# Second product of a feed-forward layer: from the planner's order to an order written out by hand, on VectorE, ScalarE and the load queue

## The chip, the cores and the metric

One NeuronCore of one Trainium2 chip runs the whole program. The metric is the device time of one execution in microseconds (us); of several executions the median is given. Engines are named as in the profile: PE (TensorE, matrix multiplications), PEld (its weight loads), DVE (VectorE), ACT (ScalarE), POOL (GpSimd) and SP (SyncE, which here only issues DMAs).

## The reference

The program is one layer of a sequence model on 512 tokens of width 2048: a state-space branch and an attention branch, merged, and then a gated feed-forward. Only the feed-forward matters here:

```python
D_MODEL, SEQ, D_FF = 2048, 512, 5632          # float32 in and out
h = rms_norm(x, norm2_w[l], RMS_EPS)
x = x + (jax.nn.silu(h @ w_ffn_gate[l]) * (h @ w_ffn_up[l])) @ w_ffn_down[l]
```

The *first product* is `h @ w_ffn_gate` and `h @ w_ffn_up`; the *second product* is the multiplication by `w_ffn_down` (5632 x 2048).

## The kernel before, in words

**Arithmetic.** Each multiplication is done by seven smaller products of operands and weights (Strassen's scheme in Winograd's form), numbered 1 to 7. Each float32 value of operands and weights is split into a high part and a rest (`whi` on ACT by `activation(Copy)`, `wlo` on DVE by a subtraction), and high x high, high x rest, rest x high are added up in PSUM. The unit of work is a *chunk* (`chunk`, L1049): one 128x1024 piece of weight (512 KB), split by ACT and DVE, then 12 multiplications of 128x128 by 128x512 on PE (line L1055 in the profile). The split results rotate through three buffers each (`halves`).

Products 1, 2 and 3 read weight blocks as they are loaded, 7, 5, 6 and 4 sums of blocks. A place A of the weights runs through these forms: block (1,1) for product 1; plus (1,2), in place, for 5; plus (2,2) for 6; plus (2,1) for 4. The other blocks are called R (2,1), r (1,2) and Q (2,2); product 7 takes r + Q, made in place of r. A += r, r += Q, A += Q are additions on DVE over 128x1024 elements. A += R is an addition of two loaded pieces or a second load of (2,1) by POOL that adds to what lies in SBUF (`pool.dma_start(..., accum_op=ALU.add)`, called the *adding load* below).

**First product.** D_FF is cut into 11 units of 512 columns, u = 0 to 10. Unit 0 runs in `seven` (L1058). Units 1 to 10 run in `units` (L1232), whose order on PE, DVE and ACT is written out step by step (`tc.manual_schedule` for these three engines): in step s PE does chunk s, ACT and DVE split the weight of step s+2, and DVE makes the sums for step s+4. What a unit leaves behind is done in `post`, a table from step to calls. The load queue (SP) is not in that order: a planner that estimates times places its loads. The results of unit u are turned by four transposes on PE (`flip_act`), split and stored in DRAM (`make`, tensor `opd`, seven operands of 512 KB for each unit) as operands of the second product.

**Second product.** It runs in six blocks of `blocks`: unit 0 alone (n = 2), then the pairs (1,2) ... (9,10) (n = 4). Each block is run for two halves v of the output rows, so there are 12 passes: 2 of 7 chunks, 10 of 14 chunks, 154 chunks in all. A pass is one call of `seven`: for each product in the order 1, 2, 7, 5, 6, 3, 4 it calls `weights` (loads and sums), `split`, `chunk` and, at the product's last chunk, `done`, which adds the two PSUM banks of the product to sums in SBUF (`acc`; the keys 11, 57, x, 53, 74). Only PE is held in program order here (`manual_schedule(engines={PE})` from the caller); DVE, ACT and SP run in the order that the planner found. The slabs with the operands (`s7`: 1 and 7, `s3`: 2 and 5, `s4`: 6 and 3, `s2`: 4) are filled at the start of a block from `opd` by 7 loads for each unit (L1525). The places A, R, Q of a block are halves of two slabs (`self.E`, `self.A`) that change roles from block to block; r takes a buffer of the ring `raw` (three). For n = 4 A += R is an adding load, in both halves v.

**The end.** The last pass is accompanied by `final` (L1496): four transposes into a PSUM bank (`flips`, banks T and O in turn), an addition of the residual by DVE and the store of a tile of 256 KB. Half v = 0 has eight such tiles during the last pass, their residual loaded by an ACT-issued DMA; of v = 1 four stand around the last two chunks and four after them. In the last block the sum x is subtracted or added in `done` directly after product 6.

Line L1350 is the helper `load` (SP), L1334 the helper `add` (DVE), L499/L500, L530/L531 and L1301/L1306 the two halves of a split, L1369 the store to `opd`, L1280 and L1556 the adding loads of the first and second product, L1229 the transposes.

Of the kernel before, what the change touches and what calls it, by code (L numbers as in the profile page):

```python
# [41 lines left out]
class Block:  # L42
    def __init__(self, ctx, tc, a):
# [12 lines left out]
        self.fp = None  # L56
        self.hook = None
# [1166 lines left out]
    def flips(self, parts):  # L1224

        self.nf += 1
        tp = self.bank("TO"[self.nf % 2])
        for h, z in enumerate(parts):
            self.nc.tensor.transpose(tp[:, h * P:(h + 1) * P], z, self.ident)  # L1229
        return tp  # L1230

    def units(self, ops, block, load, stage, stages, flip_act, make):  # L1232

        nc = self.nc
        dve, add = nc.vector, lambda o, x, y: nc.vector.tensor_tensor(o, x, y, op=ALU.add)
        NU, A, E = DFF // T, self.A, self.E
        order = ((1, 2), (7, 5, 3, 6), (4,))
        S = [(u, i, c) for u in range(1, NU) for g in order for c in range(0, 8, 2) for i in g]  # L1240
        own = {1: ("lin", "lin"), 7: ("lin", "lin"), 2: ("S", "S"), 5: ("S", "S"), 3: ("T", "O")}
        st = [{} for _ in range(NU)]

        queue = [(u, k, m, c) for u in range(1, NU) for k, m, c in
                 [(2, 1, c) for c in range(0, 8, 2)] + [(k, 2, c) for c in range(0, 8, 2) for k in (1, 2)]]
        held, w, n = [None] * 5, {}, 0

        def loads():
            nonlocal n
            while queue and held[n % 5] is None:  # L1250
                key = queue.pop(0)
                p = n % 5
                t = E[:, 2 * p - 6:2 * p - 4] if p > 2 else self.wp.tile([P, 2, T], F32, tag="raw", bufs=3, name=self.uid("raw"))
                held[p] = key
                w[key] = load(t, block(*key))
                n += 1

        def give(*key):
            held[held.index(key)] = None

        base = lambda u, c: load(A[:, c:c + 2], block(u, 1, 1, c))
        src = lambda u, i, c: A[:, c:c + 2] if i in (1, 5, 6, 4) else w[(u, *{2: (2, 1), 7: (1, 2), 3: (2, 2)}[i], c)]

        def sums(u, i, c):
            a = A[:, c:c + 2]
            if i == 7:
                add(a, a, w[u, 1, 2, c])
                add(w[u, 1, 2, c], w[u, 1, 2, c], w[u, 2, 2, c])
            elif i == 6:
                add(a, a, w[u, 2, 2, c])  # L1270

        def taken(u, i, c):
            if i == 2:
                give(u, 2, 1, c)
            elif i == 7:
                give(u, 1, 2, c)
            elif i == 3:
                give(u, 2, 2, c)
            elif i == 6:
                nc.gpsimd.dma_start(A[:, c:c + 2], block(u, 2, 1, c).rearrange("(k p) c -> p k c", p=P), accum_op=ALU.add)  # L1280
            elif i == 4 and u + 1 < NU:
                base(u + 1, c)

        post, fill, hl = {}, {}, {}
        at = lambda s, f: post.setdefault(s, []).append(f)
        for u in range(1, NU):
            s0 = 28 * (u - 1)
            for j in range(4):
                fill[s0 + 4 + j] = lambda u=u, j=j, s=s0 + 5 + j: flip_act(u - 1, j, lambda f: at(s, f))

            for f, s in zip(make(u - 1, lambda f: at(self.slot + 1, f)), range(s0 + 9, s0 + 40, 3)):
                at(s, f)
        banks = {}
        for c in range(0, 8, 2):
            base(1, c)
        for s in range(-4, len(S) + 4):
            self.slot = s
            if 0 <= s + 2 < len(S):
                x = src(*S[s + 2])
                hl[s + 2] = self.halves()  # L1300
                nc.scalar.activation(hl[s + 2][0], x, AF.Copy)  # L1301
            for f in post.pop(s, ()):
                f()
            if 0 <= s + 2 < len(S):
                hi, lo = hl[s + 2]
                self.last = nc.vector.tensor_tensor(lo, x, hi.bitcast(F32), op=ALU.subtract)  # L1306
                taken(*S[s + 2])
            if s == -4:
                loads()
            if 0 <= s + 4 < len(S):  # L1310
                sums(*S[s + 4])
            loads()
            if 0 <= s < len(S):
                u, i, c = S[s]
                if c == 0:
                    banks[i] = [self.bank(t) for t in own[i]] if i in own else banks[{6: 1, 4: 7}[i]]
                self.chunk(banks[i], ops[i], *hl.pop(s), c, 8, i in own)
                if c == 6:
                    for tt in range(2):
                        st[u][f"p{i}", tt] = banks[i][tt]  # L1320
                    for d, name in stages[i]:
                        at(s + d, lambda u=u, name=name: stage(u, st[u], name))
                if s in fill:
                    fill[s]()
        assert not post and not queue

    def ffn(self, ops, steps, x2d, out):
# [158 lines left out]
        with tc.manual_schedule(engines={mybir.EngineType.PE, mybir.EngineType.DVE, mybir.EngineType.Activation}):  # L1486
            self.units(ops, block, load, stage, STAGES, flip_act, make)
        self.ring = 0
# [3 lines left out]
        big = [self.late.tile([P, 4, 2, T], F32, tag=t, name=self.uid(t)) for t in ("s6", "s9")]  # L1492
        more = self.late.tile([P, 2, 2, T], F32, tag="s8", name=self.uid("s8"))
        acc = [{**{q: big[v][:, q_i] for q_i, q in enumerate(("11", "57", "x", "53"))}, "74": more[:, v]}
               for v in range(2)]
        def final(v, m, j):  # L1496
            t = 8 * v + 4 * m + j
            js = slice(j * P, (j + 1) * P)
            parts = [acc[v][q][:, tt, js] for q in (("11", "74"), ("53", "57"))[m] for tt in range(2)]
            tp = self.flips(parts)  # L1500
            if v:
                o = st["x2"][:, t - 8]
            else:
                o = self.work()
                nc.scalar.dma_start(o, x2d[t])
            add(dve, o, o, tp)
            nc.sync.dma_start(out[t * P:(t + 1) * P, :], o)

        both = lambda f: [lambda: (f[0](), f[1]()), lambda: (f[2](), f[3]())]
        finals = lambda v, m: [lambda j=j: final(v, m, j) for j in range(4)]  # L1510


        A, R, Q, free = self.E[:, 0:4], self.A[:, 0:4], self.A[:, 4:8], self.E[:, 4:8]
        blocks = [[0]] + [[u, u + 1] for u in range(1, NU, 2)]
        for b, units in enumerate(blocks):
# [3 lines left out]
            for tag, two_ops in (("s7", (1, 7)), ("s3", (2, 5)), ("s4", (6, 3)), ("s2", (4,))):  # L1519
                t = self.slab(tag, (P, len(two_ops), 2, n, 256), F32R)  # L1520
                for h, i in enumerate(two_ops):
                    ops[i] = t[:, h]
# [71 lines left out]
        for f in finals(1, 0):  # L1594
            f()
# [38 lines left out]
```

## Time and profile before

| | us |
|---|---|
| median of 3 executions (lowest, highest) | 2568.91 (2568.69, 2571.08) |
| the profiled execution | 2570.0 |
| its span, first to last instruction | 2568.2 |

The mean granted TensorE clock of the profiled execution is 0.993. Read the profile with the stages in mind: the first product's hand-ordered part takes the stretch up to about 2115 us of the span, the second product what follows. A busy PE row means that a multiplication was in flight, and since they overlap (0.39 us each, one started every 0.23 us) short waits can be missing from it; the spacing of starts shows them.

### The profile page before, as it was taken

To read this page: it belongs to the slowest core of one execution; us is meant where nothing else is said; L and a number is where in the kernel's file an instruction comes from. 1 tells how busy PE (TensorE), PEld (TensorE's weight loads), DVE (VectorE), ACT (ScalarE), POOL (GpSimd) and SP (SyncE) were. 2 spreads that over 40 slices of the span, in tenths; PEclk is the share of its full clock that TensorE was granted. 3 is DMA by queue.
4 is the path that set the end of the run, shared out by engine and by line. 5 is a ranking of instruction groups with operands and counts; after the bars stand their busy time and mean duration, and the time that the engine had idled before them with its cause. 6 is when DMAs were issued, how large, how long until landed. Compare 5 with 4: busy or idle time off the path is not lost.

```text
span 2568.2 us, 32111 instructions
## 1 busy us (share of the span) xinstructions
PE 2513.2 (98%) x11655; PEld 2055.4 (80%) x11655; DVE 1927.1 (75%) x3046; ACT 1145.1 (45%) x1540; POOL 316.5 (12%) x491
## 2 busy tenths in 40 slices
PE   8999999999999999999999999999999999999999
PEld 6788887877787778888788888888888887788887
DVE  7888854476778775535678787888888888788788
ACT  4133443353555553323545555555455455333332
POOL 1022310000110110000001111111111111000000
PEclk9999999999999999999999999999999999999999
DMA  6545564666852434433666666666566687767774
GB/s 191 155 131 142 149 187 154 218 216 205 269 195 97 137 117 148 160 115 131 215 180 189 168 178 176 191 197 183 165 172 180 193 254 258 249 205 234 246 231 150
DMA packets 247567, 470.86 MB, mean 183 GB/s; under 512 B 42808, under 2 KB 47224, under 8 KB 247408
## 3 DMA queue, kind: packets, MB, share of 16 engines
q1 hardware_dynamic: 185328, 331.52, 39.9%
q0 software_dynamic: 49504, 133.04, 19.2%
q10 hardware_dynamic: 12576, 4.24, 0.8%
q8 instruction: 92, 1.51, 0.2%
q14 instruction: 67, 0.55, 0.1%
HBM read 399.38 MB, written 71.96 MB: 184 GB/s over the span
## 4 chain that ended last, share of the span: by engine, by line
PE 43%; issue 39%; POOL 6%; DVE 5%; DMA 5%; ACT 1%; POOLq 0%; ACTq 0%; SPq 0%; DVEq 0%
PE lin L522 30%; PE lin L1055 5%; POOL opd L1369 3%; DMA raw<-in_w_in_dram 3%; PE S L1055 2%; DVE wlo L531 2%; POOL s L1280 1%; POOL s L1556 1%; PE S L715 1%; ACT whi L530 1%; DVE raw L1088 1%; PE S L472 1%; PE O L745 1%; PE S L414 1%; PE S L476 0%
## 5 line engine op out<-in xcount | busy, mean ns | idle before, releaser
L1055 PE MATMUL lin<-whi,s 128*128 128x512 f32 x2400 | 770.1, 392 | 1.5 <-ACT whi L530 1.5
L522 PE MATMUL lin<-s,whi 128*128 128x512 f32 x2432 | 747.5, 397 | 17.3 <-ACT s L536 7.6
L522 PEld LDWEIGHTS lin<-s,whi 128*128 128x128 f32 x2432 | 455.3, 190 | 127.7 <-issue 14.8
L1055 PEld LDWEIGHTS lin<-whi,s 128*128 128x128 f32 x2400 | 452.3, 188 | 96.0 <-ACT whi L530 2.8
L1055 PE MATMUL lin<-wlo,s 128*128 128x512 f32 x1200 | 469.8, 392 | 7.1 <-DVE wlo L531 6.9
L522 PE MATMUL lin<-s,wlo 128*128 128x512 f32 x1216 | 456.0, 394 | 0.0
L1055 PE MATMUL S<-whi,s 128*128 128x512 f32 x1328 | 436.0, 393 | 0.2 <-ACT whi L530 0.2
L500 DVE TENSOR_TENSOR wlo<-raw,whi 128x1024 fp32r<-128x1024 f32 (+1 forms) x153 | 185.7, 1215 | 214.1 <-ACT whi L499 207.3
L1301 ACT ACTIVATE whi<-s 128x1024 fp32r<-128x1024 f32 x208 | 220.9, 1062 | 273.8 <-PE lin L1055 132.0
L1306 DVE TENSOR_TENSOR wlo<-s,whi 128x1024 fp32r<-128x1024 f32 x208 | 254.2, 1222 | 110.5 <-ACT whi L1301 109.6
L499 ACT ACTIVATE whi<-raw 128x1024 fp32r<-128x1024 f32 (+1 forms) x153 | 160.9, 1052 | 360.4 <-PE lin L522 323.5
L1055 PEld LDWEIGHTS S<-whi,s 128*128 128x128 f32 x1328 | 250.5, 189 | 52.3 <-ACT whi L530 0.6
L1055 PEld LDWEIGHTS lin<-wlo,s 128*128 128x128 f32 x1200 | 226.4, 189 | 58.2 <-DVE wlo L531 12.2
L522 PEld LDWEIGHTS lin<-s,wlo 128*128 128x128 f32 x1216 | 230.4, 190 | 48.4
L1055 PE MATMUL S<-wlo,s 128*128 128x512 f32 x664 | 260.5, 392 | 8.5 <-DVE wlo L531 8.5
L530 ACT ACTIVATE whi<-s 128x1024 fp32r<-128x1024 f32 x143 | 150.9, 1060 | 228.0 <-PE lin L1055 98.6
L531 DVE TENSOR_TENSOR wlo<-s,whi 128x1024 fp32r<-128x1024 f32 x143 | 174.2, 1221 | 64.3 <-ACT whi L530 63.9
L530 ACT ACTIVATE whi<-raw 128x1024 fp32r<-128x1024 f32 x118 | 124.0, 1058 | 161.3 <-DVE raw L1088 54.0
L1369 POOL DMA_DIRECT2D opd<-wk x154 | 95.2, 618 | 671.5 <-ACT wk L1379 509.8
L531 DVE TENSOR_TENSOR wlo<-raw,whi 128x1024 fp32r<-128x1024 f32 x118 | 142.1, 1220 | 32.6 <-ACT whi L530 32.1
L1055 PEld LDWEIGHTS S<-wlo,s 128*128 128x128 f32 x664 | 125.4, 189 | 37.0 <-DVE wlo L531 11.8
L1301 ACT ACTIVATE whi<-raw 128x1024 fp32r<-128x1024 f32 x72 | 76.5, 1062 | 98.5 <-PE lin L1055 54.2
(422 smaller groups left out, 2915.3 us busy)
## 6 DMA issues: line engine op xcount, KB each, us to landing
raw<-in_w_in_dram SPq DMA_DIRECT2D x175, 512.0 KB, 4.4
opd<-wk POOLq DMA_DIRECT2D x154, 256.0 KB, 4.2
s<-opd SPq DMA_DIRECT2D x77, 512.0 KB, 8.9
s<-in_w_ffn_down_dram SPq DMA_DIRECT2D x65, 512.0 KB, 6.4
s<-in_w_ffn_gate_dram SPq DMA_DIRECT2D x60, 512.0 KB, 4.8
raw<-in_w_ffn_up_dram SPq DMA_DIRECT2D x59, 512.0 KB, 3.8
s<-in_w_ffn_gate_dram POOLq DMA_DIRECT2D x44, 512.0 KB, 6.1
raw<-in_w_out_dram SPq DMA_DIRECT2D x32, 512.0 KB, 3.7
```

Of the source, the lines that this page charges most:

```text
L414: nc.tensor.matmul(mb[:, q * 32:(q + 1) * 32], w1[:, ri, q].rearrange("p k c -> p (k c)"), self.cd[:, ri, q].rearrange("p g c -> p (g c)") ...
L472: state = lambda ri, **kw: nc.tensor.matmul(y[:, q * P:(q + 1) * P], w2[:, ri, q].rearrange("p k c -> p (k c)"), sd[:, ri, q].rearrange("p ...
L499: nc.scalar.activation(hi[:, ks], raw[:, ks], AF.Copy)
L500: nc.vector.tensor_tensor(lo[:, ks], raw[:, ks], hi[:, ks].bitcast(F32), op=ALU.subtract)
L522: nc.tensor.matmul(acc[b], l, r, start=(k == 0 and i == 0), stop=(k == nk - 1 and i == 2))
L530: ins = self.nc.scalar.activation(hi, x, AF.Copy)
L531: self.nc.vector.tensor_tensor(lo, x, hi.bitcast(F32), op=ALU.subtract)
L715: nc.tensor.matmul(sp[m], qT[ms, h, i * P:(i + 1) * P], kT[ms, h, 0:W], start=True, stop=True)
L1055: self.nc.tensor.matmul(banks[tt], l, r[:, kk, :], skip_group_check=True, start=(own and k == 0 and q == 0), stop=(k == n - 1 and q == 2))
L1301: nc.scalar.activation(hl[s + 2][0], x, AF.Copy)
L1306: self.last = nc.vector.tensor_tensor(lo, x, hi.bitcast(F32), op=ALU.subtract)
L1369: pool.dma_start(opd[u, i - 1, :, h], hl[h].bitcast(F32))
```

## The change

`units` is removed. A new method `in_order` writes out the order of units 1 to 10 and of the whole second product as one list of steps, run by a new method `pipe`; SP joins PE, DVE and ACT under `manual_schedule`. Every place of the weights (A0 to A3, E0 to E3, r0 to r2) has a list of the loads that it will hold; `give` issues the next one where the place is free. The operands of a block are no longer brought together at its start, but slab by slab, one operand and then the other two steps later, as the products of the block before (its half v = 1) are done with the slab. In second-product blocks with n = 4, A += R is a DVE addition for v = 1 (except in the last block); it stays an adding load for v = 0 and in the last block. DVE's evacuation of a product stands one step after the product's end, before the split of that step; that of product 4 two steps after. The products 7 and 5 alternate by chunk, as 1 and 2 now do in the second product; 6, 3 and 4 come one by one. The transposes of the second product use the banks S, and the residual tiles for v = 0 are loaded by SP.

The diff, cut (`...` marks what is left out):

```diff
-        tp = self.bank("TO"[self.nf % 2])
+        tp = self.bank(self.flip_banks[self.nf % 2])
...
+    def pipe(self, steps, post):
+        nc, hl, ahead = self.nc, {}, {}
+        for s, t in enumerate(steps):
+            if t.get("sums"):
+                ahead.setdefault(s - t.get("lead", 4), []).append(t["sums"])
+        s = -4
+        while s < len(steps) or post:
+            self.slot = s
+            t = steps[s + 2] if 0 <= s + 2 < len(steps) else None
+            if t:
+                x = t["x"]()
+                hl[s + 2] = hi, lo = self.halves()
+                nc.scalar.activation(hi, x, AF.Copy)
+            for f in post.pop(s, ()):
+                f()
+            if t:
+                nc.vector.tensor_tensor(lo, x, hi.bitcast(F32), op=ALU.subtract)
+                t.get("taken", lambda: None)()
+            for f in ahead.pop(s, ()):
+                f()
+            if 0 <= s < len(steps):
+                t = steps[s]
+                self.chunk(t["banks"](), t["op"](), *hl.pop(s), t["c"], t["n"], t["own"])
+                t.get("after", lambda: None)()
+            s += 1
...
-        with tc.manual_schedule(engines={mybir.EngineType.PE, mybir.EngineType.DVE, mybir.EngineType.Activation}):
-            self.units(ops, block, load, stage, STAGES, flip_act, make)
+        with tc.manual_schedule(engines={mybir.EngineType.PE, mybir.EngineType.DVE, mybir.EngineType.Activation,
+                                        mybir.EngineType.SP}):
+            self.in_order(ops, block, stage, STAGES, flip_act, make, opd, x2d, out)
+    def in_order(self, ops, block, stage, stages, flip_act, make, opd, x2d, out):
...
+        def give(name):
+            if wait.get(name):
+                key, src = wait[name].pop(0)
+                tiles[key] = place(name)
+                nc.sync.dma_start(tiles[key], two(src))
...
+        def slabs(b, tag):
...
+            for h, i in enumerate(which):
+                ops2[b, i] = t[:, h]
+                def bring(h=h, i=i):
+                    for c, u in enumerate(blocks[b]):
+                        nc.sync.dma_start(t[:, h, :, 2 * c:2 * c + 2].bitcast(F32), opd[u, i - 1])
+                at(self.slot + 2, bring) if h else bring()
...
+        def final_at(s, v, m, j, d=3):
+            st = {}
+            at(s - d, lambda: st.update(f=final(v, m, j)))
+            at(s, lambda: st.update(f=st["f"]()))
+            at(s + 1, lambda: st["f"]())
...
+        e0, a0, a3, e2 = ("E0", "E1"), ("A0", "A2"), ("A3", "A1"), ("E2", "E3")
+        roles.append(dict(A=e0, R=a0, Q=a3))
+        role = [a0, a3, e0, e2]
+        for _ in range(3, 2 * len(blocks)):
+            roles.append(dict(zip("ARQ", role)))
+            role = [role[3], role[2], role[1], role[0]]
...
+                def sums2(b, v, i, c, n):
+                    x, r, q = (tiles[b, v, z, c] for z in "ArQ")
+                    if i == 7:
+                        add(x, x, r)
+                        add(r, r, q)
+                    elif i == 6:
+                        add(x, x, q)
+                    else:
+                        add(x, x, tiles[b, v, "R", c])
+                        give(roles[2 * b + v]["R"][c // 2])
+                def taken2(b, v, i, c, n, blk, at_, rs):
+                    if i == 7:
+                        give(rs[c // 2])
+                    elif i == 3:
+                        give(at_["Q"][c // 2])
+                    elif i == 4:
+                        give(at_["A"][c // 2])
+                    elif n > 2 and (not v or b == len(blocks) - 1):
+                        if i == 2:
+                            give(at_["R"][c // 2])
+                        elif i == 6:
+                            nc.gpsimd.dma_start(tiles[b, v, "A", c], two(blk(2, 1, c)), accum_op=ALU.add)
+                def after2(b, v, i, c, n):
...
+                    at(self.slot + (2 if i == 4 and b and not last else 1), lambda: add_up(b, v, i, p))
+                    if last and i == 6:
+                        for d, q in ((2, "57"), (3, "53"), (4, "74")):
+                            at(self.slot + d, lambda q=q: less_x(v, q))
+                    if v:
+                        at(self.slot + {3: 4, 4: 5}.get(i, 1), lambda: slabs(b + 1, {7: "s7", 5: "s3", 3: "s4", 4: "s2"}.get(i)))
...
+                for g in ((1, 2), (7, 5), (6,), (3,), (4,)):
+                    for c in range(0, n, 2):
+                        for i in g:
...
+                            if i in (7, 6) or i == 4 and (n == 2 or v and not last):
+                                t["sums"] = lambda b=b, v=v, i=i, c=c, n=n: sums2(b, v, i, c, n)
+                                t["lead"] = 3 if i == 6 else 4
+                            steps.append(t)
+                if last and v:
+                    for j in range(8):
+                        final_at(s1 + 6 + j, 0, j // 4, j % 4)
+        at(s0, lambda: setattr(self, "flip_banks", "SS"))
+        turned(NU - 1, s0 + 4, 4)
...
+        for k, (v, m, j) in enumerate([(1, 1, j) for j in range(4)] + [(1, 0, j) for j in range(4)]):
+            final_at((N - 1, N - 1, N, N, N + 3, N + 3, N + 4, N + 4)[k], v, m, j, 1)
+        for c in range(4):
+            at(-4, lambda c=c: give(f"A{c}"))
+        for p in ("r0", "r1", "r2", "E0", "E1"):
+            at(-4, lambda p=p: free(p))
+        self.pipe(steps, post)
```

Here `s0` is the number of steps of the first product (280), `s1` the first step of a pass and `N` the number of all steps (434).

316 lines of the change are left out of this document (150 added, 166 removed).

## The prediction

> **What bounds the kernel now.** I read the page's first lines, then the busy time by stretch, then who PE waited for, then single instructions around the waits.
>
> ```profile
> span 2568.2 us, 32111 instructions
> PE 2513.2 (98%) x11655; PEld 2055.4 (80%) x11655; DVE 1927.1 (75%) x3046; ACT 1145.1 (45%) x1540; POOL 316.5 (12%) x491
> ```
> ```profile
> 1340.00:2114.00 774.00, 774.00 (x3492) 640.71 (x3491) 634.96 (x663) 403.50 (x486) 127.19 (x180) 1.00 0.66 187
> 2119.00:2128.00 9.00, 6.72 (x25) 4.93 (x24) 7.78 (x9) 4.14 (x6) 0.00 (x0) 0.81 0.18 60
> 2194.00:2206.00 12.00, 9.01 (x29) 6.15 (x29) 8.79 (x10) 4.20 (x5) 0.00 (x0) 0.86 0.66 214
> 2256.00:2560.00 304.00, 300.69 (x1340) 247.00 (x1339) 255.63 (x282) 112.13 (x106) 19.20 (x16) 1.00 0.67 208
> 2560.00:2568.20 8.20, 3.46 (x25) 2.39 (x23) 4.46 (x7) 0.00 (x0) 0.00 (x0) 0.97 0.57 210
> 2170.00:2190.00 20.00, 19.59 (x87) 15.71 (x86) 19.51 (x24) 8.57 (x9) 5.14 (x7) 1.00 1.05 389
> 2225.00:2240.00 15.00, 15.00 (x68) 12.42 (x67) 7.61 (x9) 5.00 (x5) 2.40 (x2) 1.00 1.02 298
> ```
> The second fence gives, for each stretch, its length, the busy time of PE, PEld, DVE, ACT and POOL, the granted clock, the DMA share and GB/s. In the hand-ordered first product (1340 to 2114) PE is busy 774.00 of 774.00 us: nothing is to be had there, and this order already keeps PE fed with DVE busy 82%. In the second product PE has gaps, and twice the clock falls (0.81, 0.86). Who it waited for after 2114.9:
>
> ```profile
> PE lin L1055 <- DVE wlo L531: 5.0, 6, 1.4
> PE S L1055 <- DVE wlo L531: 3.4, 4, 0.9
> PE lin L1055 <- ACT whi L530: 1.5, 2, 0.9
> PE O L1229 <- DVE fw L1464: 1.1, 1, 1.1
> PE O L1229 <- DVE s L1334: 1.0, 3, 0.5
> ```
> These 12.0 us are too little, since a multiplication counts 0.39 us busy but the next may start earlier. The starts tell more:
>
> ```profile
> 2101.26 0.39 PE L1055 MATMUL lin<-whi,s 128*128 128x512 f32 x1
> 2117.59 0.39 PE L1055 MATMUL S<-whi,s 128*128 128x512 f32 x1
> 2525.07 0.48 PE L1055 MATMUL S<-whi,s 128*128 128x512 f32 x1
> 2528.30 0.48 PE L1055 MATMUL lin<-whi,s 128*128 128x512 f32 x1
> 2559.68 0.39 PE L1055 MATMUL lin<-whi,s 128*128 128x512 f32 x1
> ```
> Between the first two stand six chunks of 12: 16.33 / 72 = 0.2268 us each, 2.72 us a chunk (a *step* below). Five of the six belong to unit 10, so the second product starts at 2101.26 + 60 x 0.2268 = 2114.87. Between the next two stand a chunk and one turn by four transposes: 3.23 - 2.72 = 0.51 us a turn. The last multiplication ends at 2559.68 + 0.39 = 2560.07. So the second product takes 445.2 us to its last multiplication. Its 154 chunks need 1848 x 0.2268 = 419.1, the 14 turns ahead of that point 7.1; **19.0 us are lost** to waits and the slow clock.
>
> **Where the loss comes from.** One place, DVE around 2249 (start, duration):
>
> ```profile
> 2246.21 1.22 DVE L1334 TENSOR_TENSOR raw<-raw,s 128x1024 f32<-128x1024 f32 x1
> 2247.35 0.68 DVE L1334 TENSOR_TENSOR s<-s,lin 128x512 f32<-128x512 f32 x1
> 2247.95 1.22 DVE L1334 TENSOR_TENSOR s<-s,raw 128x1024 f32<-128x1024 f32 x1
> 2249.08 0.68 DVE L1334 TENSOR_TENSOR s<-s,lin 128x512 f32<-128x512 f32 x1
> 2249.68 1.22 DVE L531 TENSOR_TENSOR wlo<-s,whi 128x1024 fp32r<-128x1024 f32 x1
> ```
> The split's rest, which PE needs next, stands behind two sums and two evacuations; PE lacked it until 2250.9. That is order, not load: in 2256 to 2560 DVE is idle for 304 - 255.6 = 48.4 us. Another place is an adding load that lands late, ACT first and then PE:
>
> ```profile
> 2199.11 2.00 ACT L530 ACTIVATE whi<-s 128x1024 fp32r<-128x1024 f32 x2 [3.04 <-DMA s<-in_w_ffn_down_dram]
> 2200.22 0.49 PE L1055 MATMUL lin<-whi,s 128*128 128x512 f32 x1 [0.94 <-ACT whi L530]
> 2201.48 0.50 PE L1055 MATMUL lin<-wlo,s 128*128 128x512 f32 x1 [0.77 <-DVE wlo L531]
> ```
>
> **The change part by part.** *First product.* PE, DVE and ACT keep their order; the loads keep theirs but for the entry. There the new order puts unit 1's four A loads ahead of r0:
>
> ```profile
> 1320.31 8.69 SPq L1350 DMA_DIRECT2D s<-in_w_ffn_gate_dram  x4
> 1331.56 1.06 ACT L1301 ACTIVATE whi<-raw 128x1024 fp32r<-128x1024 f32 x1 [1.66 <-PE lin L1055]
> ```
> The fourth A load ends its issue at 1329.0, so r0 goes out then instead of earlier. Its split (second row) feeds a multiplication two steps later, at 1337.0. With a landing after 4.6 us (median of the L1350 loads below: 5.8) r0 is there at 1333.6 to 1334.8; with 1.06 + 1.22 the pieces are ready at 1335.9 to 1337.1. Cost 0.0 to 0.1; with the operand loads' median 8.9, 3.2. Taken: 0.
>
> *DVE in a pass.*
> ```profile
> L531 DVE TENSOR_TENSOR wlo<-s,whi 128x1024 fp32r<-128x1024 f32 x130 | 158.5, 1222 | 62.0 <-ACT whi L530 61.6
> L1334 DVE TENSOR_TENSOR s<-s,lin 128x512 f32<-128x512 f32 x81 | 53.6, 680 | 1.2 <-PE lin L1055 1.2
> ```
> Back to back, the rows at 2246 start 1.14 and 0.60 apart. A pass of 14 chunks has 14 rests, 4 + 2 sums for 7 and 6 (20 x 1.14 = 22.8) and 14 evacuations (8.4): 31.2 of 38.1 us; with the new sums for 4 in v = 1, 33.5. There are eight such new additions (blocks 1 to 4, two chunks); they lie in idle time: PE pays 0, and were the cover gone, 9.1. Within a step the order is evacuation, rest, sums. The rest is ready 1.06 + 1.2 us into a step, and needed two steps (5.44) on, so DVE may lag 3.1 us. Steps 0 and 2 carry two sums: 3.42 us, and 1.2 + 1.14 follow, so the lag stays near 1.0. The worst place is the boundary: steps 278 to 282 hold the last stages of unit 10 (two 128x512 operations each, 1.2 to 1.3) beside the first sums: 1.2 + 1.14 + 2.28 in step 278, then 2.5, 2.3, 2.3, and 1.3 + 1.2 + 2.28 in step 282, 16.5 in 13.6 us. DVE ends step 282 with a lag of 2.9; the rest for step 284 is made in it at about 4.5 of the 5.44 us allowed. Cost 0 to 2.9 (the whole lag); taken 1.0, nearer to 0, since the sum leaves it 0.9 us to spare.
>
> *ACT* in a pass makes 14 high parts (1.06 each, 14.8 of 38.1 us); in the two short passes it evacuates and copies turns too, at most 3.5 us in a step, which the next step makes good. It loses eight issues of residual loads to SP. Cost 0.
>
> *Loads.* POOL issues 12 adding loads instead of 20, and its eight issues saved are off the path.
> ```profile
> SPq L1350 <- DMA s<-in_w_ffn_down_dram: 21.5, 16, 4.9
> DMA to landing us min/median/max: 3.6/5.8/14.3
> DMA to landing us min/median/max: 6.0/9.1/13.4
> s<-in_w_ffn_gate_dram POOLq DMA_DIRECT2D x44, 512.0 KB, 6.1
> s<-opd SPq DMA_DIRECT2D x77, 512.0 KB, 8.9
> ```
> (SP's longest wait for its own earlier loads; landings of L1350 and of the adding loads L1556; the adding loads of the first product; the operands.) SP now meets every wait in written order, and what follows waits behind it. Fullest are steps 7 to 11 of a pass v = 1: 14 loads of 512 KB. At 389 GB/s one takes 1.35 us, so 19 us for 13.6 us of steps. But the urgent ones stand in front: operand 1 (two), operand 2 (two), then R for the next pass. With 0.5 us to the first issue and the 2.3 by which the least landing, 3.6, exceeds 1.35, R lands near 2.8 + 5 x 1.35 = 9.6 us after step 7 begins, and ACT takes it in step 13, 16.3 us after. Cost 0.
>
> The adding loads stay in six passes. One is issued about 2.5 us into step 6, its data are needed 2.4 us ahead of step 12: 16.3 - 2.5 - 2.4 = 11.4 us against a median of 9.1 and a worst of 13.4. Cost 0 to 6 x 2.0 = 12.0. Taken 0: in the first product the distance for a unit's last chunk is the same and PE never waits, and the operand bursts now lie mostly ahead of them.
>
> *The end.* The last pass has 8 + 2 turns ahead of its last chunk as before. In step 433 three turns share two S banks: the third waits for an evacuation behind 1.2 us of sums of x and two residual additions; 1.5 us by DVE's order. After the last chunk the chain is the same: evacuation, two results, then turns and results in turn through two banks. It took 8.1 us (2560.07 to 2568.2) and stays so. The residual tiles of v = 0 rotate through five buffers, so SP's sixth load waits for the first store:
>
> ```profile
> wk<-x2d ACTq DMA_DIRECT2D x8, 256.0 KB, 6.6
> out_dram<-wk SPq DMA_DIRECT2D x8, 256.0 KB, 5.3
> ```
> The store goes out about 0.8 us into step 7 of the pass, the load lands 5.3 + 6.6 later, at 12.7; its addition is due in step 12, 5 x 3.23 = 16.2 us after step 7. Cost 0, and with the store as slow as the slowest load above (14.3 instead of 5.3) 5.5.
>
> **Sum.** 19.0 gained, less 1.5 and 1.0: span 2568.2 - 16.5 = 2551.7. The profiled execution took 2570.0, 1.8 over its span and 1.1 over the median of 2568.91; against the median, 2568.9 - 16.5 = **2552.4**.
>
> The slow clock is 3.4 of the 19.0: 0.19 x 9.0 + 0.14 x 12.0. Both spells follow gaps, so I take them with the gaps.
>
> **The rivals.** *Adding loads stay late* in the six passes, at the 0.94 + 0.77 us of the rows at 2200: 10.3 us, 2562.7. For it: their worst landing; against it: the first product.
>
> *The slow spells are not due to these gaps and stay*: 2552.4 + 3.4 = 2555.8. For it: no single PE gap quoted here is as long as 1.5 us. Against it: in 774 us without a gap the clock was 1.00. The Trainium skill, TensorE: Matmul & The Clock Gate, section "Why this matters for your kernels", bids to avoid PE gaps over about 3 us; by that bound alone these gaps would not slow the clock, and 2555.8 is its time. The trace speaks rather against it: the slow spells stand exactly where several shorter gaps lie close together.
>
> *DVE is the bound whatever its order*, since additions come to it: no change, 2569. For it: 19.51 of 20 us busy at 2170. Against it: 48.4 us idle later.
>
> *Slower: the load queue.* If R stood behind all 14 loads, and these ran at the 298 GB/s seen beside adding loads (1.76 us each), it would land 2.8 + 14 x 1.76 = 27.4 us after step 7. ACT's need at 16.3 and PE's slack of 2.9 allow 19.2; 8.2 us late in each of five blocks, 41 us, 2593. It decides against the change from 22.5 us on (3.3 late, five times the 16.5 gained). Against it: R stands fifth. The Trainium skill, DMA: Bandwidth & Descriptors, section "Anatomy of one DMA — SWDGE (gpsimd) path", says that a semaphore wait happens at the issuing sequencer before dispatch, so one late place holds up all that follows; SP's 21.5 us of waits for its own loads agree.
>
> **How the numbers follow.** Forecast 0.62, adding loads 0.14, clock 0.04, no change 0.09, slower 0.11. About 0.2% (5.1 us) is what a measurement of this kernel tells from no change; the first three lie beyond it, so faster 0.80, same 0.09, slower 0.11. Range: from 2549.5 (both losses not there, 2549.9) to 2565 (adding loads at their worst, 2564.4); outside it lie the last two cases, 0.20.
>
> **What would show it.** Right: from 2115 on, starts of multiplications 0.227 us apart across pass boundaries; no PE wait for `wlo` over 0.3 us but near the boundary and in the last steps; granted clock 1.00; the last multiplication near 2543.5; 12 adding loads. Wrong: PE waits for ACT or DVE that repeat once a pass (their releaser, a load or DVE's own order, names the rival), or any wait in the first product, which would come from SP's order.

## The result, and the profile after

| | median us (lowest, highest), executions | ratio to before, 95% interval |
|---|---|---|
| before | 2569.20 (2568.05, 2571.86), 6 | |
| after | 2553.01 (2548.48, 2558.93), 6 | 0.9937 [0.9921, 0.9952] |

The change is faster by 16.2 us, near the predicted 2552.4. The ratios in this text leave out slow executions; there was one, of e12_sums, with 7031 us. The profiled execution took 2552.43 us. The page's first lines, then busy time by stretch of the changed kernel (length; busy time of PE, PEld, DVE, ACT, POOL; granted clock; DMA share; GB/s):

```profile
span 2550.6 us, 32136 instructions
PE 2506.2 (98%) x11655; PEld 2053.8 (81%) x11655; DVE 1934.6 (76%) x3054; ACT 1144.1 (45%) x1540; POOL 307.6 (12%) x483
```
```profile
1338.00:2109.00 771.00, 771.00 (x3478) 638.42 (x3477) 633.69 (x662) 401.68 (x484) 126.58 (x179) 1.00 0.66 187
2109.05:2542.50 433.45, 428.65 (x1907) 353.48 (x1906) 377.28 (x414) 176.47 (x185) 22.73 (x27) 1.00 0.67 221
2542.50:2550.65 8.15, 3.38 (x25) 2.32 (x22) 4.45 (x7) 0.00 (x0) 0.00 (x0) 0.84 0.52 193
```
The same stretch of the kernel before, cut by its own starts:

```profile
2114.87:2560.07 445.20, 433.85 (x1907) 353.78 (x1906) 369.59 (x405) 177.42 (x185) 31.60 (x34) 0.99 0.70 224
```
PE still has no gap in the first product. The second product takes 433.45 us to its last multiplication instead of 445.20: 11.75 shorter, not 16.5. DVE works 7.7 us more, POOL 8.9 less. The other 5.8 us of the span (17.6 in all) come before 2109. The first product's ten units take 780.78 us in every kernel here whose DVE order is written out. Unit 0 took 79.7 us against 81.8; over the twelve profiles of the new code and its variants it took 79.7 to 81.2, over the two of before 81.8 and 81.5, so some 1.4 us seem to be the change's (in unit 0 PE waits 3.2 us for `wlo` in before, 1.6 in after; why the planner's order came out better there was not looked into). The remaining 3.7 lie ahead of unit 0, where the order of instructions is the same in both. The start of unit 0 moved between 1244.0 and 1252.3 over the fourteen profiles; before's spent 27.3 us of that stretch at half clock, after's 20.5, the others 6.8 to 20.5.

Who PE waited for in the second product of after, and its late starts one by one (start, duration; in brackets the idle time before and what ended it):

```profile
PE S L1230 <- DVE wk L1430: 4.2, 3, 2.1
PE T L1056 <- DVE wlo L1253: 0.4, 1, 0.4
PE lin L1056 <- DVE wlo L1253: 0.2, 1, 0.2
```
```profile
2111.78 0.39 PE L1056 MATMUL S<-whi,s 128*128 128x512 f32 x1
2174.09 0.50 PE L1056 MATMUL lin<-wlo,s 128*128 128x512 f32 x1 [0.23 <-DVE wlo L1253]
2202.18 0.50 PE L1056 MATMUL T<-wlo,s 128*128 128x512 f32 x1 [0.38 <-DVE wlo L1253]
2529.75 0.65 PE L1230 MATMUL S<-ident,big 128*128 128x128 f32 x4 [0.96 <-DVE wk L1430]
2535.69 0.66 PE L1230 MATMUL S<-ident,big 128*128 128x128 f32 x4 [2.09 <-DVE wk L1430]
2537.49 0.83 PE L1230 MATMUL S<-ident,big 128*128 128x128 f32 x4 [1.15 <-DVE wk L1430]
2542.11 0.39 PE L1056 MATMUL lin<-whi,s 128*128 128x512 f32 x1
```
By the spacing of starts, two waits for `wlo` are left, both in block 1 (0.39 and 0.54 us, 65 and 93 us into the second product), and three turns of the last pass wait for a bank (1.12, 2.26, 1.32). At the boundary from the first to the second product there is none. All waits of PE on ACT, 0.7 to 1.1 us each in before, are gone.

The gain lies in two stretches and is partly given back in a third. A pass of 14 chunks without a loss takes 38.08 us, and the ten turns of the last pass 5.1. Against that, before lost 12.5 us in the first 28 chunks of the second product (block 0 and the first pass of block 1), 6.3 in the next eight passes and 0.3 in the last pass; after lost 0.6, 0.7 and 6.2. So the change won 17.6 us ahead of the last pass and gave back 5.8 in it.

**Why the last turns are late.** SP's queue and its wait at the 2 MB load, one POOL issue, the landing of what was issued from 2514.9 to 2516, the landings of that line's eight residual loads (L1590), and the DVE operation that waited (after):

```profile
SPq L1672 <- PE lin L1056: 28.1, 1, 28.1
2512.86 0.37 SPq L1672 DMA_DIRECT2D s<-x2d  x1
2514.67 0.34 SPq L1597 DMA_DIRECT2D out_dram<-wk  x1
2515.06 0.86 SPq L1590 DMA_DIRECT2D wk<-x2d  x1
2513.93 1.20 POOL L1655 DMA_DIRECT2D s<-in_w_ffn_down_dram  x1 [33.65 <-issue]
s<-in_w_ffn_down_dram POOLq DMA_DIRECT2D x1, 512.0 KB, 10.7
wk<-x2d SPq DMA_DIRECT2D x1, 256.0 KB, 13.9
DMA to landing us min/median/max: 3.0/6.5/13.9
2529.01 0.69 DVE L1430 TENSOR_TENSOR wk<-wk,S 128x512 f32<-128x512 f32 x1 [1.96 <-DMA wk<-x2d]
```
At 2512.86 SP issues one load of 2 MB (the residual of half v = 1, not needed before the last chunks). SP had stood 28.1 us at it, until PE was done with the slab that it fills, and the fifth residual tile stood behind it in the written order. That tile, 256 KB, then takes 13.9 us, where the fastest of the eight took 3.0; the adding load issued at 2513.93 takes 10.7, and ACT waits 4.4 us for it. DVE waits for the tile (1.96 us) and for ACT's splits in its fixed order, the turns share two S banks that DVE empties, and PE loses 4.7 us, and 1.55 more to a slow clock (a *spell*: a stretch at half clock, here 3.41 us). Which of the late loads counts most these lines don't tell; the experiments below do in part.

### The profile page after: what moved, and what is told of

It is laid out like the page before. It is cut to its first block, busy times and chain, and to the rows that moved or that the text cites. A ratio compares the mean times of both kernels' runs of the same rounds, so it can differ in the third digit from the quotient of the medians.

```text
span 2550.6 us, 32136 instructions
## 1 busy us (share of the span) xinstructions
PE 2506.2 (98%) x11655; PEld 2053.8 (81%) x11655; DVE 1934.6 (76%) x3054; ACT 1144.1 (45%) x1540; POOL 307.6 (12%) x483
## 4 chain that ended last, share of the span: by engine, by line
PE 80%; issue 11%; DVE 4%; DMA 4%; ACT 1%; POOL 1%; ACTq 0%; SPq 0%; POOLq 0%; DVEq 0%
PE lin L1056 27%; PE lin L523 27%; PE S L1056 12%; PE T L1056 5%; PE O L1056 5%; DMA raw<-in_w_in_dram 1%; PE S L716 1%; PE O L746 1%; PE S L473 1%; DMA out_dram<-wk 1%; PE S L477 1%; DVE s L1430 0%; PE S L415 0%; DVE wlo L532 0%; DVE wlo L501 0%
## 5 line engine op out<-in xcount | busy, mean ns | idle before, releaser
L1249 ACT ACTIVATE whi<-s 128x1024 fp32r<-128x1024 f32 x340 | 360.0, 1062 | 480.1 <-PE lin L1056 225.1
L1253 DVE TENSOR_TENSOR wlo<-s,whi 128x1024 fp32r<-128x1024 f32 x340 | 414.7, 1222 | 156.0 <-ACT whi L1249 154.8
L1056 PE MATMUL S<-whi,s 128*128 128x512 f32 x976 | 323.4, 393 | 0.2 <-ACT whi L531 0.2
L523 PEld LDWEIGHTS lin<-s,wlo 128*128 128x128 f32 x1216 | 230.0, 189 | 48.3
L1056 PEld LDWEIGHTS S<-whi,s 128*128 128x128 f32 x976 | 183.8, 188 | 38.4 <-ACT whi L531 0.6
L1056 PE MATMUL S<-wlo,s 128*128 128x512 f32 x488 | 190.9, 391 | 2.9 <-DVE wlo L532 2.9
L1056 PE MATMUL T<-whi,s 128*128 128x512 f32 x400 | 139.7, 390 | 0.0
L1056 PE MATMUL O<-whi,s 128*128 128x512 f32 x400 | 139.4, 389 | 0.0
L1253 DVE TENSOR_TENSOR wlo<-raw,whi 128x1024 fp32r<-128x1024 f32 x94 | 114.8, 1222 | 31.9 <-ACT whi L1249 30.8
L532 DVE TENSOR_TENSOR wlo<-raw,whi 128x1024 fp32r<-128x1024 f32 x95 | 114.5, 1221 | 31.0 <-ACT whi L531 30.4
```

The costliest lines, as they stand in the source:

```text
L523: nc.tensor.matmul(acc[b], l, r, start=(k == 0 and i == 0), stop=(k == nk - 1 and i == 2))
L532: self.nc.vector.tensor_tensor(lo, x, hi.bitcast(F32), op=ALU.subtract)
L1056: self.nc.tensor.matmul(banks[tt], l, r[:, kk, :], skip_group_check=True, start=(own and k == 0 and q == 0), stop=(k == n - 1 and q == 2))
L1249: nc.scalar.activation(hi, x, AF.Copy)
```

## The experiments

Lengths below are the second product's, from its first multiplication to the end of the span: 453.4 before, 441.6 after. Spans of one kernel differ by several us, mostly ahead of unit 0, so this length tells more than one time. What the product pays behind its last multiplication is about 8.1 in all of them but the two with other banks (7.1) and e9 (8.6).

**Both kernels again.**

> The changed kernel once more, unaltered. In the first profiled pair the second product took 441.5 us (2109.1 to 2550.6) against 453.3 before (2114.9 to 2568.2), so 11.8 us of 17.6; the other 5.8 had been gained before the second product began, in stages whose instruction order is the same in both kernels up to unit 0 of the first product. Theory: those 5.8 us are mostly the difference of one execution from another (about 4.4) and the second product's 11.8 is the change's own. Expected: median 2553 +- 3, the second product again 441 to 443 us, its start anywhere from 2106 to 2117. Rival: the changed kernel is really faster in the stages before; then the start is again at 2109 +- 1.

> The kernel before once more, unaltered, for a second profile. Theory: its second product is as steady as that of the changed kernel, which took 441.6 and 442.2 us in two executions: 453.4 +- 0.7 us again, with 19 us of loss in it, while the start of the second product may move by some us, since the stages before it have slow-clock spells in varying number. Rival: the second product itself varies by several us from one execution to the next; then it is off by more than 2.

```profile
2106.49:2540.50 434.01, 429.13 (x1907) 353.54 (x1906) 377.73 (x415) 176.45 (x185) 22.70 (x27) 1.00 0.67 221
```
```profile
2108.99:2552.55 443.56, 432.25 (x1907) 352.51 (x1906) 369.64 (x405) 177.47 (x185) 31.60 (x34) 1.00 0.71 225
```
The first row is the changed kernel, the second the kernel before, on two other chips: 442.2 and 451.7. After repeats; before is 1.7 shorter, 1.0 below what I expected, with one slow spell of the clock instead of two. The second product gained 11.8 in one pair and 9.6 in the other, about 10.5. On the chip of the first row the times stand at 2552.01 against 2565.77, ratio 0.9947 [0.9935, 0.9960].

**The end.** e3_end loads residual tiles earlier, moves the 2 MB load three steps on, and gives the last turns more banks; e5_res is its loads alone.

```diff
-                o = self.work()
+                o = self.E[:, 4 + t] if t < 4 else self.work()
-                        x2.append(self.slab("s7", (P, 8, T), F32))
-                        nc.sync.dma_start(x2[0], ...)
+                        def residual(): ...        # the same two lines
+                        at(self.slot + 3, residual)
-                        final_at(s1 + 6 + j, 0, j // 4, j % 4)
+                        final_at(s1 + 6 + j, 0, j // 4, j % 4, 6 + j if j < 4 else 5 + j)
 # e3_end only:
...
+        at(len(steps) - 8, lambda: self.last_banks.extend(["S"] * 8 + ["lin", "lin", "T", "O"]))
-            final_at((N - 1, N - 1, N, N, ...)[k], v, m, j, 1)
+            final_at((N - 1, N - 1, N - 1, N - 1, ...)[k], v, m, j, 1)
```

> Only the last pass differs from the changed kernel: the residual tiles of v = 0 are loaded at its first two steps (four of them into a free place of the weights, so that no load waits for a store), the 2 MB load of x2 goes out three steps later, behind the adding loads, and the last four turns of the half tiles (1,1) stand ahead of the last chunk with banks of their own (lin, lin, T, O). Theory: of the 7.2 us that PE still loses in the second product, 6.2 lie in the last pass: 0.96 + 2.09 + 1.15 us of waits for DVE, which waited for residual loads behind the 2 MB load and for two banks, and 1.7 us of slow clock after them. They go, and 1 us of the tail goes too: second product 441.5 - 6.2 - 1 = 434 us, about 0.28% faster than the changed kernel. Rival: the adding loads, which landed 10.7 us after their issue, are what is late; then the waits move to the product 4's chunks and the second product stays over 438.

> Of the altered end only the loads: residual tiles of v = 0 loaded at the first two steps of the last pass and the 2 MB load of x2 three steps later; the turns and their banks as in the changed kernel. Theory: the waits on late loads (1.1 us in step 431 and about half of the 2.3 + 1.3 us and of the slow clock in step 433) go, the wait of the third turn for its bank stays at 1.5 us as worked out: second product 441.6 - 4 = 437.5. Rival: the banks are all of it, 440 and more.

e3_end by stretch and its PE waits in it; then the PE waits of e5_res:

```profile
2109.20:2537.70 428.50, 427.89 (x1915) 353.19 (x1914) 378.79 (x417) 176.51 (x185) 22.69 (x27) 1.00 0.68 224
PE T L1057 <- DVE wlo L1254: 0.4, 1, 0.4
PE lin L1057 <- DVE wlo L1254: 0.2, 1, 0.2
```
```profile
PE S L1230 <- DVE wk L1430: 0.5, 1, 0.5
PE T L1056 <- DVE wlo L1253: 0.4, 1, 0.4
PE lin L1056 <- DVE wlo L1253: 0.2, 1, 0.2
```
e3_end takes 435.6 (434 expected), e5_res 436.2 (437.5): the loads alone bring 5.4 of the 6.0. The two banks that I had taken for the cause (1.5 us in the prediction) cost 0.7 once the loads are there in time. So it is the loads; but e5_res moves several at once. The residual tiles go out earlier, and the 2 MB load goes out behind the adding loads, which then land after 6.8 and 6.9 us instead of 10.7 and 11.3. The slow spell went with the waits. In time e3_end has 2546.93, ratio to before 0.9928 [0.9916, 0.9941].

**Which engine's written order matters.** Engines were taken out of `manual_schedule`, so that the planner places their instructions, with the new list of steps as it is:

```diff
-  engines={PE, DVE, Activation, SP}
+  engines={PE, DVE, Activation}      # e4_sp_free
+  engines={PE, Activation, SP}       # e6_dve_free
+  engines={PE}                       # e9_pe_only
```

> The changed kernel without SP in the written order: the planner places the loads, all else is the same. Theory: the gain comes from DVE's order, the load order follows from when places come free, so the second product stays within 3 us of 441.5 (a little better at the end if the planner puts the residual loads earlier). Rival: the written load order carries the gain; then waits of 1 to 2 us a pass return, 450 us and more.

> The changed kernel without DVE in the written order: the planner orders DVE, PE, ACT and SP keep theirs. Theory: rests that stand behind sums and evacuations return as PE waits for wlo, 0.5 to 1.5 us at many pass starts: second product 447 to 456 us, and some loss in the first product's units too. Rival: the two-step lead of ACT and the loads is enough and DVE's order does not matter: 441 to 443.

> The changed kernel with the same list of steps, but only PE held to it: the planner orders DVE, ACT and SP. Theory: the list itself (splits two steps, sums four steps ahead, operands brought slab by slab) gives the planner what the second product needs: second product 442 to 447 us, with the first product longer by 20 us and more as with DVE alone left to the planner (805 instead of 781). Rival: the fixed order of ACT and SP is what keeps the lead; then waits return at the pass starts, 450 us and more, near the 453 of before.

First and second product of e6_dve_free, then of e9_pe_only:

```profile
1327.51:2132.58 805.07, 789.44 (x3522) 644.50 (x3520) 635.79 (x670) 406.39 (x491) 126.31 (x179) 1.00 0.64 182
2132.58:2566.75 434.17, 428.90 (x1907) 353.55 (x1906) 379.79 (x413) 177.04 (x185) 22.69 (x27) 1.00 0.67 221
```
```profile
1325.14:2139.27 814.13, 790.95 (x3522) 643.77 (x3520) 636.55 (x671) 412.52 (x490) 127.24 (x180) 1.00 0.62 179
2139.27:2576.78 437.51, 431.57 (x1907) 355.48 (x1906) 380.08 (x411) 177.48 (x185) 22.14 (x26) 0.99 0.67 218
```
| | second product | its first 28 chunks | next eight passes | last pass | first product |
|---|---|---|---|---|---|
| without a loss | | 78.2 | 304.6 | 43.2 | |
| before, its repeat | 453.4, 451.7 | 90.7, 89.5 | 311.0, 311.0 | 43.5, 43.1 | 780.8 |
| after, its repeat | 441.6, 442.2 | 78.8, 79.2 | 305.3, 305.3 | 49.4, 49.5 | 780.8 |
| e4_sp_free | 445.3 | 82.4 | 306.4 | 48.3 | 780.8 |
| e6_dve_free | 442.3 | 80.9 | 304.6 | 48.6 | 805.1 |
| e9_pe_only | 446.1 | 88.6 | 304.9 | 44.1 | 814.1 |

The three stretches go from start to start of their first multiplications (the last pass to the end of its last one); with what follows they make up the second product.

By the totals, the new list with only PE in written order keeps about 6 of the 10.5 us, giving up the load queue's order costs 3 to 4, just over what I expected (2557.53 against 2552.01 in the times), and giving up DVE's costs nothing: my theory for e6 (447 to 456) fell. But the totals hide opposite parts. In the eight middle passes the list alone does it: e9 takes 304.9, without a loss. In the first 28 chunks (block 0 and the first pass of block 1) the written orders count: e9 gives back 9.4 to 9.8 of the 10 to 12 us won there, e4 3.2 to 3.7, e6 1.7 to 2.2. In the last pass they cost: after loses 6.2, e4 5.1, e6 5.4, e9 0.9. DVE's written order is worth 24.3 us in the first product (2576.36 against 2552.01 in the times), where before had it already.

These runs also bear on the end. In e4, with DVE's order written, DVE waits for no residual tile, and PE still loses 3.6 us in the last turns, besides the slow spell; the adding loads land after 10.6 and 11.3 us as in after. In e6, with SP's order written, DVE waits 4.3 us for a residual tile. In e9 loads are as late (adding loads 11.5 and 12.6, a residual tile behind the 2 MB load 15.4), in before too (adding loads 9.7 and 11.8), and little is lost. So late loads alone do not make the loss, and the late residual tile is not all of it; what the written orders put behind a late load seems to decide. That was not tried by itself.

**Additions against adding loads.** e7_adding keeps all else of the change and makes A += R by POOL again in the passes v = 1 too (`elif n > 2:` for the adding load, sums for 4 only where `n == 2`).

> The changed kernel with the eight new DVE additions undone: A += R is an adding load by POOL in both halves v, as before the change (20 adding loads instead of 12). Theory: DVE has the time for the additions and the adding loads have the time to land, so either way PE waits for neither: second product 441.5 to 443 us. Rivals: adding loads late by 1.7 us a pass cost 4 x 1.7 = 7 us more, 449; or DVE is the bound, and taking the additions from it gains, 439 or less.

PE and ACT waits of e7_adding, ahead of the last pass's end and in the whole second product; below them ACT's wait of that kind in after:

```profile
PE lin L1056 <- DVE wlo L1253: 2.0, 5, 0.8
ACT whi L1249 <- DMA s<-in_w_ffn_down_dram: 47.4, 16, 4.8
```
```profile
ACT whi L1249 <- DMA s<-in_w_ffn_down_dram: 17.1, 7, 4.4
```
446.6: 4.4 to 5.0 longer than after, where I had expected at most 1.4. ACT waits for 16 loads instead of 7, and once in each of blocks 1 to 4, in the pass v = 1, this reaches PE (1.03, 0.46, 0.66, 0.35 us by the starts). These four passes take 3.5 us more than in after, the last pass 1.4 more. So in the middle passes the eight additions on DVE are a good part of what the list brings.

**Slack.** e8_gaps repeats the rest at the first chunk of product 3, pass v = 0, four to seven extra times in blocks 1 to 4.

```diff
+                    for _ in range(1 + t.get("more", 0)):
+                            if b in (1, 2, 3, 4) and not v and (i, c) == (3, 0):
+                                t["more"] = 3 + b
```

> The changed kernel with one PE gap in each of four passes (v = 0 of blocks 1 to 4): at the first chunk of product 3 the rest is made 5, 6, 7 and 8 times over instead of once, 4 to 7 x 1.14 us more on DVE. The slack found is about 3.3 us, so PE should wait 1.2, 2.4, 3.5 and 4.6 us, alone each time. Theory, from the traces: the clock falls to a half for one 3.4 us spell wherever PE is idle for most of a 3.4 us stretch, so after the gaps of 3.5 and 4.6 surely, after 2.4 perhaps, after 1.2 not: 11.7 us of waits and 3 to 5 us of slow clock, second product about 457. Rival (only a gap of over 3 us slows the clock): after the last two only, 455.

DVE's repeats in block 2, PE's late start behind them, and two stretches of slow clock that followed gaps:

```profile
2257.84 8.65 DVE L1254 TENSOR_TENSOR wlo<-s,whi 128x1024 fp32r<-128x1024 f32 x7
2265.41 0.79 PE L1056 MATMUL T<-wlo,s 128*128 128x512 f32 x1 [4.81 <-DVE wlo L1254]
2264.52:2271.35 6.83, 5.94 (x14) 4.68 (x15) 4.30 (x5) 0.80 (x1) 0.00 (x0) 0.50 0.67 199
2179.19:2186.02 6.83, 4.72 (x11) 3.75 (x12) 6.08 (x7) 0.00 (x0) 0.00 (x0) 0.50 0.57 192
```
The gaps are 5.10, 4.97, 6.23 and 7.49 us, not 1.2 to 4.6. One repeat takes 8.65 / 7 = 1.24 us, not 1.14, and the seven extra ones (8.7 us) leave a gap of 7.5: in blocks 2 to 4 DVE's slack is 1.2 us at that place, not 3.1. In block 1 it has none (four repeats, 5.0 us, leave a gap of 5.1); there DVE still splits unit 10's operands, and there stand the two waits for `wlo` in after. Each gap brought 6.8 us at half clock. The second product took 476.1 us, not 457: of the 34.5 more than after 23.8 are the gaps, nearly all the rest slow multiplications. Since all gaps were over 3 us, this run doesn't tell whether shorter ones would have done so.

**How far ahead.** e10_lead1 lists the splits of the passes of 14 chunks one step ahead instead of two; e11_two_buffers leaves the list and gives those passes two split buffers instead of three (`self.halves(t["n"] != 4)`).

> The changed kernel with the weights of the ten long passes split one step ahead of their multiplications instead of two; everything else as it was. With DVE left to the planner the second product stayed at 442.3, so the order of DVE within a step is not what carries it. Theory now: it is the lead. With one step (2.72 us) a rest that stands behind an evacuation is ready 1.2 + 1.14 us into its step, and behind two sums of the step before later still (0.7 to 1.0 us of lag): waits of 0.3 to 1 us at three to five steps of a pass, 10 to 40 us in all, second product 450 to 480. Rival: the three buffers of the split, not the place in the list, give the lead; then ACT and DVE run ahead anyway and it stays at 442 to 446.

> The changed kernel with two instead of three buffers for the split halves in the ten long passes; order and leads unaltered. With the split listed one step ahead instead of two the second product stayed at 443.9, so the place in the list is not what gives the lead. Theory: the third buffer is. With two, a high part cannot begin before PE has left the chunk two back, so it is ready 1.06 us into the step before its use and the rest 1.2 us after it, or 2.3 to 3.6 us with an evacuation or a sum ahead of it, against 2.95 us: waits of 0.3 to 1 us at several steps of a pass, second product 452 to 475. Rival: two are enough; 442 to 444.

e11_two_buffers, its stretch and PE's waits in it:

```profile
2106.90:2579.90 473.00, 441.68 (x1907) 349.86 (x1906) 380.03 (x414) 177.41 (x185) 22.69 (x27) 1.00 0.62 202
PE S L1056 <- DVE wlo L1253: 12.6, 9, 2.1
PE lin L1056 <- DVE wlo L1253: 9.2, 22, 1.1
PE S L1230 <- DVE wk L1430: 4.8, 3, 2.3
PE T L1056 <- DVE wlo L1253: 3.6, 3, 2.0
```
e10 takes 444.0, 2 us more than after: the theory that the listed distance carries the gain (450 to 480) fell. e11 takes 481.1, 39 more and above the range that I gave. What lets ACT and DVE run ahead is the third buffer; with two, a split must wait for PE to leave the step before last, and what DVE does beside it (evacuations, sums) shows as waits. Before had three buffers too, so this is not the change's gain, but both orders rest on it.

**The two left waits.** e12_sums is e3_end with the sums for product 6 listed four steps ahead, as the others are.

> The kernel with the altered end (loads and banks), and the sums A += Q for product 6 made four steps ahead instead of three in the long passes. In the gap experiment DVE had 1.4 us to spare at the first chunk of product 3 instead of the 3.1 worked out, because the sum for product 6, its high part on ACT, its rest and the next sum follow each other one by one on two engines. One step earlier that chain starts before it is needed: the wait of 0.39 us at 64.9 us into the second product goes, the one of 0.54 at 93.0 (sums for product 7) stays. Second product 435.6 - 0.4 = 435.2 us; no difference to the kernel with the altered end that times can tell, some 0.7% faster than the kernel before. Rival: the evacuations behind the sums are pushed back and other waits come up; 436 and more.

It takes 436.1. The two waits of block 1 changed (0.35 and 0.33 us) and a new one of 0.47 came: nothing gained. Its times stand at 2546.11, ratio 0.9921 [0.9903, 0.9939], which e3_end's interval overlaps.

## Why the prediction was right, point by point

**The total** came so near by luck: the second product gained 11.75 us instead of 16.5 (4.75 missing), made up by 5.8 us ahead of it that the prediction didn't have, of which some 1.4 seem the change's and the rest the execution's. By medians the two chips gave 16.2 and 13.8 us; some 10.5 of that is the second product and perhaps 1.4 unit 0. Where the other 2 to 4 come from is open.

**Right.** *First product* at no cost (780.78 us, no wait). *Boundary*: 1.0 taken, out of 0 to 2.9; nothing measured. *ACT*: no PE wait for it. *Adding loads* of the six passes: none kept a chunk waiting, and ACT waited 17.1 us for them where it had 40.5:

```profile
L1655 POOL DMA_DIRECT2D s<-in_w_ffn_down_dram x12: 1190/1204/1240, 2170.3 to 2517.3; - x12
DMA to landing us min/median/max: 6.1/6.2/11.3
```
Their median fell from 9.1 to 6.2 in after; the rival with 2562.7 did not come. Nor did *the load queue*: SP waited long in its order, yet no operand or weight load reached PE late. The two adding loads of the last pass (10.7 and 11.3) lay just inside the 11.4 us that the sum allowed them.

```profile
SPq L1459 <- DVE wlo L1253: 244.7, 56, 14.3
```
*The clock*: both spells of before went with their gaps, as the sum had it (see below for the rule behind); a new one came with the new gaps in the last pass.

**Mis-sized.** *The end* is the term that failed: 1.5 us taken, 4.7 of waits and 1.55 of slow clock measured, 6.25; the missing 4.75 are this. The prediction looked at the five buffers and at the banks, but its sum has the 2 MB load nowhere: neither that SP would stand at it with a residual tile behind, nor that what is issued after it lands late. The first store took 13.1 us, where 5.3 were taken. e5_res shows that moving the loads brings 5.4 us back. *DVE in a pass* was taken at 0, and two waits came in block 1, 0.39 + 0.54 = 0.93 us; that this nearly equals the 1.0 of the boundary is chance. The sign "no PE wait for `wlo` over 0.3 us but near the boundary and in the last steps" failed there. Where e8 measured it, DVE's slack was 1.2 us or none, not 3.1.

**Wrong in the cause.** I put before's loss down to DVE's order ("That is order, not load"), at a place in the middle passes. There the new list takes the loss away with DVE's written order or without it (305.3 and 304.6 us), and the additions in place of eight adding loads are a good part of that. How the rest divides among splits two ahead, sums ahead and slabs brought one by one was not tried. And two thirds of the loss, 12.5 of 19.0 us, lay in the first 28 chunks. The gain there needs the written orders: SP's is worth 3.2 to 3.7 us of it, DVE's 1.7 to 2.2, and giving up these two and ACT's together costs 9.4 to 9.8. ACT's alone was not tried.

## What to carry to other kernels

When loads get a fixed place in one queue, ask of each large one what small, urgent load comes behind it: here a 2 MB load with time to spare went out first, and putting the urgent loads ahead of it brought 5.4 us. Before paying for a written order, take the engines out of it one at a time, and compare stretch by stretch: one order (DVE's) was worth 24 us in the first product and nothing in the total of the second, and a total can hide a gain in one stretch and a loss in another. How far ACT and DVE ran ahead here hung on the number of buffers (39 us), hardly on the step in which the work is listed (2 us).

## What the runs showed of the hardware

**The clock is decided on a fixed grid.** In every trace here the starts of the slow spells lie a whole number of 3.413 us apart, and what decides, but for a few windows, is how much PE was busy in the grid window before. Windows ahead of a spell in before (two) and after, then one without a spell in e11_two_buffers:

```profile
2120.52:2123.93 3.41, 1.13 (x6) 0.58 (x5) 3.41 (x5) 0.96 (x2) 0.00 (x0) 1.00 0.02 5
2199.03:2202.44 3.41, 1.70 (x7) 1.00 (x6) 2.24 (x2) 2.00 (x2) 0.00 (x0) 1.00 0.31 120
```
```profile
2534.42:2537.83 3.41, 0.99 (x7) 0.76 (x8) 3.41 (x7) 0.00 (x0) 0.00 (x0) 1.00 0.71 264
```
```profile
2161.78:2165.19 3.41, 1.86 (x8) 1.54 (x9) 3.41 (x6) 0.78 (x1) 1.08 (x2) 1.00 1.06 389
```
Over all fourteen traces, of the windows at full clock with PE busy under 1.8 us (about half), 55 of 62 were followed by half clock (the other seven had 1.56 to 1.77); of some 10,250 with more, 11 (1.81 to 2.52). So two gaps of 1.0 to 1.4 us in one window can slow the next (2123.93 and 2202.44 in before), while e11's gaps of 2.2 us, with PE busy on both sides, did not: it has one spell in its second product, in the last turns. The Trainium skill, TensorE: Matmul & The Clock Gate, section "Why this matters for your kernels", bids to avoid gaps over about 3 us. The gaps of e8 agree with it; before and after lost clock without any gap that long, so here the measurement says idle share of a window, not length of a gap. That several short gaps near each other do it, as the prediction argued, is thereby borne out.

**A load behind a large one.** 256 KB issued 2.2 us behind 2 MB on the same queue landed after 13.9 us, against 3.0 at the least. Adding loads of 512 KB, from POOL, landed later too: after 10.7 us for the one issued 1.1 us behind the 2 MB load, after 6.8 for the same one in e5_res, where the 2 MB load came after it.
